# Up phase of a gated MLP: stored first products written back into the accumulating bank, first weights earlier, rows by halves

## The chip, the cores and the metric

One core of a Trainium2 chip. The metric is the device time of one execution in microseconds; the time before is the median of three runs, 2032.83 us (2030.95 to 2035.71).

## The reference

One layer of a decoder trunk over 1024 positions of 1024 channels in fp32: a token-mixing part (a conformer convolution branch and a Mamba-2 branch, gated and projected by `w_o`), a layer norm, a convolutional gated MLP, a layer norm. The change lies in the MLP and in the seams on both its sides:

```python
def conv_ffn(h, w_up, dw_w, dw_b, w_down):
    u = causal_dwconv(h @ w_up, dw_w, dw_b)      # 1024 -> 2 x 2816 columns, 3 taps
    gate, val = jnp.split(u, 2, axis=-1)
    return (jax.nn.silu(gate) * val) @ w_down    # 2816 -> 1024

h = layer_norm(DN_ALPHA * h + mix, ln1_g[l], ln1_b[l])
ffn = conv_ffn(h, w_ffn_up[l], ffn_dw_w[l], ffn_dw_b[l], w_ffn_down[l])
h = layer_norm(DN_ALPHA * h + ffn, ln2_g[l], ln2_b[l])
```

## The kernel before

Every fp32 product is made of three matmuls (`mm3`, lines 166 to 168): each operand is split into a rounded part (a ScalarE cast) and the rest (a VectorE subtraction), and three of the four cross products are added in one bank of PSUM. There are eight banks, four of tag "acc" (`bank(1)`) and four of tag "sm" (`bank(0)`).

The mixing part takes the positions in two halves, up to about 1350 us. Then come the stages of the change.

- `ffn_blocks` (to about 1391 us) opens the pool "trans" on the left side of the core's memory. Its first tiles are `ln1_g`, `ln1_b` and three buffers "row" of 4,096 bytes per partition each, then `h1raw` and the small `ts` tiles. `out_proj_pairs` projects the last four row blocks in two pairs and norms them (L717, L207, L227, L230); `block_sums` transposes each block (L758) and forms the sums and differences of blocks that a seven-product (Strassen-like) scheme needs, written into `h1b1`, `h1b2` and `h1s1` to `h1s3` (L763, L764; POOL does some of the sums, L788, L794).
- `up_first`: for the first eight pairs of columns (`LEAD = 8`) the two products that need only the early positions are made ahead, since they don't depend on the last rows: product with `b11`, copied out of the bank (L823) into a tile of the pool "firsts" (right side) and stored to `first_scr` in HBM, then the product with `b21` added onto the same bank, copied and stored again. Their weights pass through `weights()` (L152 to L155): a load into `wst` (three buffers, tag "st"), a cast and a split into `wsp` (three buffers).
- `up_rest` (about 1406 to 1794 us), 22 pairs. `up_weights` loads two weight tiles (`ra` L831 into "st", `rb` L836 into "raw", three buffers), forms four sums (L840 to L843) and splits (`split_pair`, L740, L741) into `wsp` (`w24`, `w10`) and the pool "up" (`w3`). Each pair then has five products of 12 matmuls (t2, t3, t1, t4, b22), and pairs from the ninth on the two first ones as well. In the first eight pairs the stored sums are loaded again (L867, L868), and three VectorE additions (L871, L877, L885) join them to what is in the banks; in the later ones everything accumulates in the bank and ScalarE copies it out (L860, L865, L875, L883). L878 and L880 form `uv` on VectorE in all pairs. Then a 3-tap convolution: a first tap on ScalarE into a tile "o" (L891, three buffers), two on VectorE (L895), SiLU (L905), the gating (L906), and for every second pair four sums (L920 to L923). The results go to HBM by POOL's queue (L916, L918, L924, L925).
- `down` (about 1794 to the end): seven products over eleven blocks each, weights through `load` (L979 and after) into `w_dn` tiles. `c3` and the 1024 rows of the residual (`rows`) take over the two big tiles. `load_rows` brings the rows by POOL's queue (L946); the first five `c3` blocks come by POOL's queue a second time (L982). `ln2`'s two rows are loaded by SP ahead of it all (L203).

The order on each engine is made by a planner from estimated times: among what is ready it takes what stands first in program order, where `high_priority(offset=n)` counts as n instructions earlier. A tile that lies where tiles of a closed pool lay waits for those tiles (`reuse_waits="tile"`). The pools stack up from the left and from the right side; "up" opens after "trans" has closed and so begins at the same address.

Of the kernel before, what the change touches and what calls it, by code (L numbers as in the profile page):

```python
# [8 lines left out]
F32 = mybir.dt.float32  # L9
F32R = mybir.dt.float32r  # L10
AF = mybir.ActivationFunctionType
ALU = mybir.AluOpType
# [4 lines left out]
P = 128  # L17
D = 1024
T = 1024
# [37 lines left out]
def kernel(  # L57
# [756 lines left out]

    def up_first(fp, bl, j):


        w = weights(wup[2 * j], f"ue{j}")
        ps = bank(1)
        for q, block in enumerate(("b11", "b21")):  # L820
            product(ps, lambda i: w[:, i, q * HALF : (q + 1) * HALF], bl[block], q == 0)
            f = fp.tile([P, HALF], F32, tag="first", bufs=4, name=f"first{q}_{j}")
            A.copy(f, ps)  # L823
            A.dma_start(first_scr[j][q], f)
# [23 lines left out]

    def up_rest(upp, us, bl, j, before):

        ue, w24, w10, w3 = up_weights(upp, j)
        ug, uv = us[2 * j % 3], us[(2 * j + 1) % 3]
        s = upp.tile([P, HALF], F32, tag="s", bufs=2, name=f"s{j}")
        early, late = slice(2, 2 + HALF), slice(2 + HALF, 2 + T)
        ps, pz = bank(1 if ue else 0), bank(0)
        if ue:
            product(ps, lambda i: ue[:, i, :HALF], bl["b11"], True)
            A.copy(s, ps)  # L860
            py = bank(1)
            product(py, lambda i: ue[:, i, HALF:], bl["b21"], True)
            V.tensor_tensor(out=ug[:, early], in0=s, in1=py, op=ALU.add)
            product(ps, lambda i: w24[:, i, :HALF], bl["t2"], False)
            A.copy(s, ps)  # L865
        else:
            SY.dma_start(s, first_scr[j][0])  # L867
            SY.dma_start(ug[:, early], first_scr[j][1])  # L868
            pu = bank(0)
            product(pu, lambda i: w24[:, i, :HALF], bl["t2"], True)  # L870
            V.tensor_tensor(out=s, in0=s, in1=pu, op=ALU.add)  # L871
        product(pz, lambda i: w3[:, i], bl["t3"], True)
        product(ps, lambda i: w10[:, i, :HALF], bl["t1"], not ue)
        if ue:
            A.copy(uv[:, late], ps)  # L875
        else:
            V.tensor_tensor(out=uv[:, late], in0=s, in1=ps, op=ALU.add)  # L877
        V.tensor_tensor(out=uv[:, late], in0=pz, in1=uv[:, late], op=ALU.subtract)  # L878
        product(pz, lambda i: w10[:, i, HALF:], bl["t4"], False)
        V.tensor_tensor(out=uv[:, early], in0=pz, in1=s, op=ALU.subtract)  # L880
        product(ps, lambda i: w24[:, i, HALF:], bl["b22"], False)
        if ue:
            A.copy(ug[:, late], ps)  # L883
        else:
            V.tensor_tensor(out=ug[:, late], in0=s, in1=ps, op=ALU.add)  # L885
        os = []
        j = j // 2 + j % 2 * NK
        for jj, u in ((j, ug), (NF + j, uv)):
            o = upp.tile([P, T], F32, tag="o", bufs=3, name=f"fo{jj}")
            wc = PC_FW + 3 * jj  # L890
            A.activation(  # L891
                out=o, in_=u[:, 2 : 2 + T], func=AF.Identity, scale=pc[:, wc + 2 : wc + 3]
            )
            for k in range(2):
                V.scalar_tensor_tensor(  # L895
                    out=o,
                    in0=u[:, k : k + T],
                    scalar=pc[:, wc + k : wc + k + 1],
                    in1=o,
                    op0=ALU.mult,  # L900
                    op1=ALU.add,
                )
            os.append(o)
# [22 lines left out]

    def down(upp, dp, g, b):

# [14 lines left out]

        def load_rows(ts):
            for t in ts:
                G.dma_start(rs[t], h1_scr[t * P : (t + 1) * P, :])  # L946

        E, L = slice(0, HALF), slice(HALF, D)

# [13 lines left out]
        def load(p, k):  # L963
# [12 lines left out]
            with tc.high_priority(offset=4000):  # L976
# [3 lines left out]
                if p == 0 and k < EARLY:  # L980
                    SY.dma_start(w_st, a11)
                    G.dma_start(c3[k], a11)  # L982
                elif p == 0:
# [77 lines left out]
        def four(t):  # L1061
            more(Y[t], rs[t], L, ALU.add)
            ln_part(dp, rs[t], sts[t], 1)
            ln_out(upp, t, rs[t], g, b, sts[t])

        def three(t):
            own(X[t], rs[4 + t], E, ALU.add)
            ln_part(dp, rs[4 + t], sts[4 + t], 0)
            ln_out(upp, 4 + t, rs[4 + t], g, b, sts[4 + t])

# [46 lines left out]
    with pool("trans") as tp:  # L1117
        bl = ffn_blocks(tp, qp, mixT)
    with pool("firsts", side="right") as fp:
        for j in range(LEAD):  # L1120
            up_first(fp, bl, j)
    upp = ctx.enter_context(pool("up"))
    us = [upp.tile([P, T + 32], F32, name=f"u{i}") for i in range(3)]
    for u in us:
        G.memset(u[:, :2], 0.0)
# [106 lines left out]
```

## Time and profile before

| | |
|---|---|
| runs | 2035.71, 2032.83, 2030.95 us; median 2032.83 |
| profiled execution | 2035.35 us, span 2033.6 us |
| TensorE busy | 1978.0 us (97%), mean granted clock 0.99 |
| VectorE, ScalarE, GpSimd busy | 1710.7 (84%), 1001.8 (49%), 171.9 us (8%) |
| HBM | 222.36 MB read, 49.55 MB written, 134 GB/s over the span |
| TensorE idle, 1400.5 to 1405.8 us | 5.3 us |
| TensorE waits on VectorE's L877 in the first eight pairs | 7.0 us in 3 |
| TensorE waits on ScalarE's L875 at 1804 us | 5.39 us in 1 |

PE is TensorE, PEld its weight loads, DVE VectorE, ACT ScalarE, POOL GpSimd, SP the queue that issues most loads. Times are microseconds from the start of the span. A row of the timeline gives start, duration, engine, line, operation, output and inputs, and in brackets the idle time before it and what ended it. A row of the groups gives count, busy time and mean nanoseconds, then the idle time ahead of them by releaser. A row of the waits gives engine, line, what it waited for, and total, number and longest.

### The profile page before, as it was taken

What the parts mean: (1) busy time and instruction counts of PE and PEld (TensorE: products, weight loads), DVE (VectorE), ACT (ScalarE), POOL (GpSimd) and SP (SyncE); (2) the same over time, 40 slices, a digit from 0 to 9 for tenths busy, and PEclk for the clock granted to TensorE, in tenths of its full rate; (3) what the DMA queues carried; (4) which work ended last, traced back from release to release, by engine and by line L of the source; (5) the groups of instructions that cost most, each with busy time, mean ns of one, the idle gap of its engine ahead of it and who ended that gap; (6) DMA issues with size and microseconds to landing.
All of it is one profiled execution on the core that took longest, in us unless ns stands there. A gap on an engine that the chain in (4) does not pass through costs nothing.

```text
span 2033.6 us, 24571 instructions
## 1 busy us (share of the span) xinstructions
PE 1978.0 (97%) x9164; PEld 1628.0 (80%) x9164; DVE 1710.7 (84%) x2285; ACT 1001.8 (49%) x1448; POOL 171.9 (8%) x141
## 2 busy tenths in 40 slices
PE   6999999999999999999999999998899999989998
PEld 6888887888788888888888888887778888777886
DVE  7599999989766869999998976596998788777868
ACT  4465654556453356665454645364334445443432
POOL 2010101001400000100100130010000000010000
PEclk9999999999999999999999999999999999999999
DMA  6212233332546522222423354565342232377563
GB/s 219 93 63 94 79 102 106 99 104 101 174 133 216 195 88 77 88 85 75 127 86 107 109 166 138 188 234 202 130 153 106 99 109 99 109 258 264 175 224 109
DMA packets 97303, 273.51 MB, mean 134 GB/s; under 512 B 11168, under 2 KB 11168, under 8 KB 97184
## 3 DMA queue, kind: packets, MB, share of 16 engines
q1 hardware_dynamic: 87696, 242.06, 35.9%
q0 software_dynamic: 7184, 25.69, 3.3%
q10 hardware_dynamic: 2304, 4.20, 0.6%
q8 instruction: 72, 1.18, 0.2%
q14 instruction: 47, 0.39, 0.1%
HBM read 222.36 MB, written 49.55 MB: 134 GB/s over the span
## 4 chain that ended last, share of the span: by engine, by line
PE 66%; DVE 24%; DMA 4%; issue 4%; ACT 1%; SPq 0%; DVEq 0%; ACTq 0%
PE acc L166 17%; PE acc L168 17%; PE acc L167 17%; DVE c L420 8%; PE sm L166 3%; PE sm L167 3%; PE sm L168 3%; DVE xbc L375 2%; DMA dr<-b_scr 1%; PE acc L357 1%; PE sm L534 1%; DVE fo L895 1%; DMA st_wo<-wo 1%; PE sm L515 1%; DVE w_so L155 1%
## 5 line engine op out<-in xcount | busy, mean ns | idle before, releaser
L420 DVE SCALAR_TENSOR_TENSOR c<-v,pc,c 128x512 f32<-128x512 f32 x480 | 375.3, 805 | 7.6 <-ACT c L409 6.1
L478 POOL TENSOR_TENSOR au<-seg_mv,head_of 128x1024 fp32r<-128x1024 f32 x32 | 76.3, 2383 | 962.2 <-PE sm L487 730.4
L166 PE MATMUL acc<-hT,w_c 128*128 128x512 f32 x352 | 141.1, 401 | 0.0
L167 PE MATMUL acc<-hT,w_c 128*128 128x512 f32 x352 | 140.7, 400 | 0.0
L168 PE MATMUL acc<-hT,w_c 128*128 128x512 f32 x352 | 138.5, 393 | 0.0
L895 DVE SCALAR_TENSOR_TENSOR fo<-u,pc,fo 128x1024 f32<-128x1024 f32 x88 | 111.5, 1279 | 8.5 <-ACT fo L891 7.8
L375 DVE SCALAR_TENSOR_TENSOR xbc<-u,pc,xbc 128x512 f32<-128x512 f32 x144 | 109.7, 774 | 0.7 <-ACT xbc L373 0.5
L167 PE MATMUL acc<-w_z,hT 128*128 128x512 f32 x256 | 100.9, 394 | 0.0
L166 PE MATMUL acc<-w_z,hT 128*128 128x512 f32 x256 | 100.9, 401 | 0.0
L168 PE MATMUL acc<-w_z,hT 128*128 128x512 f32 x256 | 100.7, 396 | 0.0
L1021 ACT CAST w_dn<-dr 128x1024 fp32r<-128x1024 f32 (+1 forms) x73 | 60.8, 842 | 77.7 <-DVE dr L951 31.5
L154 ACT CAST w_c<-st_c 128x1024 fp32r<-128x1024 f32 x50 | 52.5, 1051 | 86.8 <-PE acc L168 66.1
L1022 DVE TENSOR_TENSOR w_dn<-dr,w_dn 128x1024 fp32r<-128x1024 f32 (+1 forms) x73 | 69.6, 963 | 17.6 <-ACT w_dn L1021 17.5
L167 PEld LDWEIGHTS acc<-hT,w_c 128*128 128x128 f32 x352 | 66.2, 188 | 16.8 <-issue 3.8
L168 PEld LDWEIGHTS acc<-hT,w_c 128*128 128x128 f32 x352 | 66.1, 188 | 16.0 <-issue 2.6
L166 PEld LDWEIGHTS acc<-hT,w_c 128*128 128x128 f32 x352 | 66.1, 188 | 15.9 <-issue 2.6
L155 DVE TENSOR_TENSOR w_c<-st_c,w_c 128x1024 fp32r<-128x1024 f32 x47 | 60.6, 1289 | 20.2 <-ACT w_c L154 20.2
L166 PE MATMUL acc<-h1s,w_s 128*128 128x512 f32 x168 | 66.6, 397 | 5.7 <-ACT u L875 5.7
L166 PE MATMUL acc<-h1b,w_ue 128*128 128x512 f32 x176 | 68.9, 392 | 2.6 <-ACT w_ue L740 1.4
L166 PE MATMUL sm<-h1b,w_s 128*128 128x512 f32 x176 | 70.3, 400 | 0.0
L167 PE MATMUL sm<-h1b,w_s 128*128 128x512 f32 x176 | 70.3, 399 | 0.0
L168 PE MATMUL sm<-h1b,w_s 128*128 128x512 f32 x176 | 69.9, 397 | 0.0
(352 smaller groups left out, 5811.1 us busy)
## 6 DMA issues: line engine op xcount, KB each, us to landing
st_c<-wcol SPq DMA_DIRECT2D x50, 512.0 KB, 3.5
st_z<-wz SPq DMA_DIRECT2D x32, 512.0 KB, 3.4
st_wo<-wo SPq DMA_DIRECT2D x24, 512.0 KB, 3.8
ra<-wup SPq DMA_DIRECT2D x22, 512.0 KB, 3.6
rb<-wup SPq DMA_DIRECT2D x22, 512.0 KB, 3.4
t_scr<-fo POOLq DMA_DIRECT2D x22, 512.0 KB, 4.2
dr<-t_scr SPq DMA_DIRECT2D x44, 256.0 KB, 3.4
dr<-wdown SPq DMA_DIRECT2D x38, 256.0 KB, 3.8
```

Source lines behind the costliest of these rows:

```text
L154: A.copy(w[:, 0, :], st)
L155: (eng or V).tensor_tensor(out=w[:, 1, :], in0=st, in1=w[:, 0, :].bitcast(F32), op=ALU.subtract)
L166: TE.matmul(ps, wa(0), xa(0), start=start, stop=False, skip_group_check=more)
L167: TE.matmul(ps, wa(0), xa(1), start=False, stop=False, skip_group_check=more)
L168: TE.matmul(ps, wa(1), xa(0), start=False, stop=stop, skip_group_check=more)
L357: TE.matmul(ps[:, ts], w[:, i, k * P : (k + 1) * P], hT[:, j, k, ts], start=n == 0 and k == 0, stop=n == 2 and k == KD - 1,)
L375: V.scalar_tensor_tensor(out=o, in0=u[:, k : k + HALF], scalar=pc[:, wc + k : wc + k + 1], in1=o, op0=ALU.mult, op1=ALU.add,)
L420: V.scalar_tensor_tensor(out=accs[i], in0=v[:, k : k + HALF], scalar=pc[:, wc + k : wc + k + 1], in1=accs[i], op0=ALU.mult, op1=ALU.add,)
L478: G.tensor_tensor(out=au, in0=seg_mv[:, c, :].unsqueeze(1).to_broadcast([P, 8, P]), in1=head_of[:, g, :].unsqueeze(2).to_broadcast([P, 8, P]),
L895: V.scalar_tensor_tensor(out=o, in0=u[:, k : k + T], scalar=pc[:, wc + k : wc + k + 1], in1=o, op0=ALU.mult, op1=ALU.add,)
L1021: A.copy(w[:, 0, cs], src)
L1022: V.tensor_tensor(out=w[:, 1, cs], in0=src, in1=w[:, 0, cs].bitcast(F32), op=ALU.subtract)
```

## The change

- `up_first` copies its sums into the halves of the three `u` tiles of the pool "up" (`us[j % 3]`) instead of into "firsts", which is gone. "up" and the clearing of the `u` tiles move ahead of it.
- For j = 6 and 7 the weights are loaded and split by hand into two "o" tiles of "up" each, not into `wsp`. `up_weights(upp, 0)` is called ahead of them and its result handed to the first `up_rest`.
- In the first eight pairs ScalarE copies the stored first sum into the accumulating bank (`A.copy(ps, s)`), t2 is added onto it, and the rest goes as in the later pairs: L871, L877 and L885 become ScalarE copies. The loads of the stored sums get a priority of 2,500. `ps` is always an "acc" bank, and the bank `pu` is gone.
- "o" has four buffers instead of three.
- In `down` the rows are loaded by halves of columns, in four groups at k = 4 of products 0, 1, 2 and 4 (before: whole rows, two groups at k = 2 of 0 and 2). `ln2`'s rows come by POOL's queue with the third group, into "o" tiles. The first five `c3` blocks are copied on POOL from the tile just loaded, not loaded again.

```diff
-    def up_first(fp, bl, j):
-        w = weights(wup[2 * j], f"ue{j}")
+    def up_first(upp, us, bl, j):
+        if j < LEAD - 2:
+            t = weights(wup[2 * j], f"ue{j}")
+            w = [t[:, i, :] for i in range(2)]
+        else:
+            with tc.high_priority(offset=4000):
+                st = wst.tile([P, D], F32, tag="st", name=f"st_ue{j}")
+                SY.dma_start(st, wup[2 * j])
+                w = [upp.tile([P, D], F32R, tag="o", bufs=4, name=f"ue{i}_{j}") for i in range(2)]
+                A.copy(w[0], st)
+                V.tensor_tensor(out=w[1], in0=st, in1=w[0].bitcast(F32), op=ALU.subtract)
...
-            f = fp.tile([P, HALF], F32, tag="first", bufs=4, name=f"first{q}_{j}")
+            f = us[j % 3][:, 2 + q * HALF : 2 + (q + 1) * HALF]
             A.copy(f, ps)
             A.dma_start(first_scr[j][q], f)
...
-        ue, w24, w10, w3 = up_weights(upp, j)
+        ue, w24, w10, w3 = ws or up_weights(upp, j)
...
-        ps, pz = bank(1 if ue else 0), bank(0)
+        ps, pz = bank(1), bank(0)
...
-            product(ps, lambda i: w24[:, i, :HALF], bl["t2"], False)
-            A.copy(s, ps)
         else:
-            SY.dma_start(s, first_scr[j][0])
-            SY.dma_start(ug[:, early], first_scr[j][1])
-            pu = bank(0)
-            product(pu, lambda i: w24[:, i, :HALF], bl["t2"], True)
-            V.tensor_tensor(out=s, in0=s, in1=pu, op=ALU.add)
+            with tc.high_priority(offset=2500):
+                SY.dma_start(s, first_scr[j][0])
+                SY.dma_start(ug[:, early], first_scr[j][1])
+            A.copy(ps, s)
+        product(ps, lambda i: w24[:, i, :HALF], bl["t2"], False)
+        A.copy(s, ps)
         product(pz, lambda i: w3[:, i], bl["t3"], True)
-        product(ps, lambda i: w10[:, i, :HALF], bl["t1"], not ue)
-        if ue:
-            A.copy(uv[:, late], ps)
-        else:
-            V.tensor_tensor(out=uv[:, late], in0=s, in1=ps, op=ALU.add)
+        product(ps, lambda i: w10[:, i, :HALF], bl["t1"], False)
+        A.copy(uv[:, late], ps)
...
-        if ue:
-            A.copy(ug[:, late], ps)
-        else:
-            V.tensor_tensor(out=ug[:, late], in0=s, in1=ps, op=ALU.add)
+        A.copy(ug[:, late], ps)
...
-            o = upp.tile([P, T], F32, tag="o", bufs=3, name=f"fo{jj}")
+            o = upp.tile([P, T], F32, tag="o", bufs=4, name=f"fo{jj}")
...
-        def load_rows(ts):
-            for t in ts:
-                G.dma_start(rs[t], h1_scr[t * P : (t + 1) * P, :])
+        def load_rows(p):
+            t0, cs = {0: (0, E), 1: (0, L), 2: (4, L), 4: (4, E)}[p]
+            for t in range(t0, t0 + 4):
+                G.dma_start(rs[t][:, cs], h1_scr[t * P : (t + 1) * P, cs])
+            if p == 2:
+                for n, start in (("g", RW_2G), ("b", RW_2B)):
+                    r = upp.tile([P, D], F32, tag="o", bufs=4, name=f"ln2_{n}")
+                    G.dma_start(r, prow[start : start + D].partition_broadcast(P))
+                    gb.append(r)
...
-                    G.dma_start(c3[k], a11)
+                    G.tensor_copy(c3[k], w_st)
...
-                if k == 2 and p in (0, 2):
-                    load_rows(range(2 * p, 2 * p + 4))
+                if k == 4 and p in (0, 1, 2, 4):
+                    load_rows(p)
...
-    with pool("firsts", side="right") as fp:
-        for j in range(LEAD):
-            up_first(fp, bl, j)
     upp = ctx.enter_context(pool("up"))
     us = [upp.tile([P, T + 32], F32, name=f"u{i}") for i in range(3)]
     for u in us:
         G.memset(u[:, :2], 0.0)
+    for j in range(LEAD):
+        if j == LEAD - 2:
+            ws = up_weights(upp, 0)
+        up_first(upp, us, bl, j)
     before = None
     for j in range(NF):
-        before = up_rest(upp, us, bl, j, before)
+        before, ws = up_rest(upp, us, bl, j, before, ws), None
     ffn_stack.close()
     dp = ctx.enter_context(pool("down", side="right"))
-    g, b = row(dp, RW_2G, D, "ln2_g"), row(dp, RW_2B, D, "ln2_b")
-    down(upp, dp, g, b)
+    down(upp, dp)
```

More of the change, by code (lines that the diff above doesn't have):

```diff
@@ L813, in ffn_blocks @@
         }
-    def up_first(fp, bl, j):
-        w = weights(wup[2 * j], f"ue{j}")
+    def up_first(upp, us, bl, j):
[9 more added lines that the diff above has]
+                V.tensor_tensor(out=w[1], in0=st, in1=w[0].bitcast(F32), op=ALU.subtract)
         ps = bank(1)
         for q, block in enumerate(("b11", "b21")):
-            product(ps, lambda i: w[:, i, q * HALF : (q + 1) * HALF], bl[block], q == 0)
-            f = fp.tile([P, HALF], F32, tag="first", bufs=4, name=f"first{q}_{j}")
+            product(ps, lambda i: w[i][:, q * HALF : (q + 1) * HALF], bl[block], q == 0)
+            f = us[j % 3][:, 2 + q * HALF : 2 + (q + 1) * HALF]
             A.copy(f, ps)
@@ L847, in up_weights, with up_rest @@
         return ue, w24, w10, w3
-    def up_rest(upp, us, bl, j, before):
-        ue, w24, w10, w3 = up_weights(upp, j)
+    def up_rest(upp, us, bl, j, before, ws):
+        ue, w24, w10, w3 = ws or up_weights(upp, j)
         ug, uv = us[2 * j % 3], us[(2 * j + 1) % 3]
@@ L925, in up_rest, with down @@
         G.dma_start(t41_scr[j - NK], a)
-    def down(upp, dp, g, b):
+    def down(upp, dp):
         LAST, EARLY = 8, 5
@@ L1063, in four @@
             ln_part(dp, rs[t], sts[t], 1)
-            ln_out(upp, t, rs[t], g, b, sts[t])
+            ln_out(upp, t, rs[t], *gb, sts[t])
         def three(t):
@@ L1068, in three @@
             ln_part(dp, rs[4 + t], sts[4 + t], 0)
-            ln_out(upp, 4 + t, rs[4 + t], g, b, sts[4 + t])
+            ln_out(upp, 4 + t, rs[4 + t], *gb, sts[4 + t])
         products = (
```

1 line of the change is left out of this document (added).

## The prediction

> **What bounds the kernel now.** I read the page's busy shares first, then the busy time of each engine by stretches, then TensorE's waits in the stretches where it was idle.
>
> ```profile
> span 2033.6 us, 24571 instructions
> PE 1978.0 (97%) x9164; PEld 1628.0 (80%) x9164; DVE 1710.7 (84%) x2285; ACT 1001.8 (49%) x1448; POOL 171.9 (8%) x141
> ```
>
> TensorE is the bound over the whole span, so only its idle or slow stretches can be won. The change touches three places; these are their stretches (columns: window, then busy us of PE, PEld, DVE, ACT, POOL, granted clock, DMA share, GB/s):
>
> ```profile
> 1350.00:1400.50 50.50, 49.34 (x224) 40.13 (x222) 39.21 (x55) 27.58 (x46) 9.14 (x9) 1.00 0.61 218
> 1400.50:1405.80 5.30, 0.04 (x1) 0.00 (x0) 3.59 (x6) 2.86 (x5) 0.00 (x0) 0.92 0.89 307
> 1405.80:1411.50 5.70, 5.66 (x13) 4.46 (x14) 5.03 (x7) 1.99 (x2) 0.00 (x0) 0.50 0.74 231
> 1405.80:1531.00 125.20, 117.07 (x479) 93.77 (x480) 113.62 (x141) 45.69 (x46) 6.61 (x12) 0.95 0.41 143
> 1430.00:1531.00 101.00, 93.31 (x390) 74.79 (x389) 96.66 (x118) 39.88 (x40) 6.61 (x12) 0.97 0.44 154
> 1600.00:1700.00 100.00, 100.00 (x439) 81.99 (x438) 83.36 (x94) 50.22 (x60) 5.87 (x11) 1.00 0.31 108
> 1800.00:1810.00 10.00, 5.73 (x18) 4.64 (x19) 6.89 (x6) 3.79 (x5) 0.54 (x1) 0.66 0.34 134
> 1830.00:1840.00 10.00, 7.50 (x29) 5.48 (x28) 5.29 (x9) 3.32 (x6) 1.07 (x2) 0.92 1.03 403
> ```
>
> In 1600 to 1700 a 512-column matmul takes 100/439 = 0.228 us. By that measure the eight first pairs (8 x 60 = 480 matmuls in 1405.8 to 1531) need 109.3 us and take 125.2: 15.9 too many. VectorE is busy 96.66 of 101 us there, against 83 of 100 later. Before them lie 5.3 idle us, and the 5.7 us after these run at half clock (13 matmuls, 2.9 us lost). In the down phase 1800 to 1810 has 18 matmuls and 1830 to 1840 has 29, for 44 each: 5.9 and 3.4 us lost.
>
> **a. First columns: the new staging place.** Before, `up_first` copied its sums into the pool "firsts" on the right side, which nothing else held. Now it copies into `us`, the first 3 x 4,224 bytes per partition of the pool "up". That pool opens where "trans" has just closed, and trans begins with `ln1_g`, `ln1_b` (4,096 bytes each) and three `row` buffers. So `us[0]` lies on `ln1_g` and the start of `ln1_b`, `us[1]` on `ln1_b` and the head of a row buffer, `us[2]` on row buffers. These are read until the last layer norm of `out_proj_pairs`:
>
> ```profile
> 1353.34 0.39 PE L166 MATMUL acc<-h1b,w_ue 128*128 128x512 f32 x1
> 1356.81 0.58 ACT L823 COPY first<-acc 128x512 f32<-128x512 f32 x1
> 1360.06 1.21 DVE L155 TENSOR_TENSOR w_ue<-st_ue,w_ue 128x1024 fp32r<-128x1024 f32 x1
> 1365.49 1.18 DVE L155 TENSOR_TENSOR w_ue<-st_ue,w_ue 128x1024 fp32r<-128x1024 f32 x1
> 1371.95 1.22 DVE L155 TENSOR_TENSOR w_ue<-st_ue,w_ue 128x1024 fp32r<-128x1024 f32 x1
> 1373.07 1.03 PE L758 MATMUL sm<-ident,r 128*128 128x128 f32 x8
> 1373.08 1.27 DVE L230 SCALAR_TENSOR_TENSOR r<-r,rs_o,ln_b 128x1024 f32<-128x1024 f32 x1
> 1383.08 0.17 POOL L1125 MEMSET u<- 128x2 f32 x3
> 1390.26 0.69 DVE L764 TENSOR_TENSOR h1b<-ts,h1b 128x512 fp32r<-128x512 f32 x1 [0.69 <-ACT h1b L763]
> ```
>
> The first sum was copied out at 1356.81; its new place is free at 1373.08 + 1.27 = 1374.4. The two weight splits at 1365.49 and 1371.95 belong to columns 3 and 4, whose buffer (three in `wsp`) is not free until column 0 is done, so they fall behind and the norm ends 2.3 us sooner, at 1372.1; with the copy (0.58) TensorE can go on at about 1372.8. Until then it can do the first product of columns 0, 1 and 2 (three weight buffers; the third split ends at 1361.3). Before, (1372.8 - 1353.34) / (12 x 0.228 = 2.73) = 7.1 products were done by then, so 4.1 are late: 11.3 us. One of two groups of eight row transposes (1.03 us) moves into the gap: +10.3. The gap is over 5 us, so by the 1405.8 row half clock follows: +2.9. Sum of a: **+13.2**.
>
> **b. From first columns to pairs.** The gap comes from the weights of pair 0, which could take a `wsp` buffer only when the last columns gave theirs back:
>
> ```profile
> 1397.48 0.50 PE L166 MATMUL acc<-h1b,w_ue 128*128 128x512 f32 x1 [1.17 <-ACT first L823]
> 1405.84 0.79 PE L166 MATMUL sm<-h1s,w_s 128*128 128x512 f32 x1 [5.30 <-ACT w_s L740]
> ```
>
> Columns 6 and 7 now use two "o" tiles each, pair 0's weights take `wsp` buffers after columns 3 to 5, some 8 us ahead of need (`wup` loads for it move ahead of two others on SP; at a DMA share of 0.61 that costs nothing). Columns 6, 7 make the same casts and splits; their "o" tiles lie on `h1raw`, free before 1391, and are due after 1400. So the 5.3, the half clock (2.9) and the wait of 1.17, which pair 0's products can fill, go: **-9.4**.
>
> **c. The first eight pairs.** Removed from VectorE are the three additions of each pair, added to ScalarE are four copies of 512 columns:
>
> ```profile
> L871 DVE TENSOR_TENSOR s<-s,sm 128x512 f32<-128x512 f32 x8 | 5.5, 683 | 0.1
> L877 DVE TENSOR_TENSOR u<-s,sm 128x512 f32<-128x512 f32 x7 | 4.8, 684 | 0.6 <-PE sm L168 0.6
> L885 DVE TENSOR_TENSOR u<-s,sm 128x512 f32<-128x512 f32 x7 | 4.8, 684 | 2.8 <-PE sm L168 2.6
> L860 ACT COPY s<-acc 128x512 f32<-128x512 f32 x9 | 5.3, 589 | 12.6 <-PE acc L168 12.6
> L891 ACT ACTIVATE fo<-u,pc 128x1024 f32<-128x1024 f32 x14 | 16.0, 1151 | 13.4 <-DVE fo L923 8.7 <-DMA t_scr<-fo 3.6 <-DVE u L880 0.6
> PE sm L166 <- DVE u L877: 7.0, 3, 3.9
> SPq L868 <- DVE fo L895: 38.7, 6, 10.6
> ```
>
> VectorE loses 24 x 0.684 = 16.4 us: 113.6 becomes 97.2, or 89% of 109. ScalarE gains 32 x 0.59 = 18.9 (the copy into PSUM has no row; 0.58 to 0.62 are the nearest): 45.7 becomes 64.6, 59%. TensorE's order in a pair is now that of pairs 8 to 21, which run with no idle at VectorE 83%. Of the 15.9 us too many, 2.9 are b's half clock; of the other 13.0 I let 3.5 stay, since VectorE remains fuller than later: **-9.5** (ends: -13, and +2 in the rival below). The copy into the bank waits for the load of `s` alone, which SP issues earlier (up to 2,500 instructions); on SP the loads of `ra`, `rb` stand behind it and behind `u`'s, which waited 38.7 us in six times already without TensorE waiting for a load. I cost that at nothing: weights come a pair ahead; without this cover a late load is some 3 us each.
>
> **d. Start of the down phase.**
>
> ```profile
> 1786.23 2.71 POOL L982 DMA_DIRECT2D c<-wdown  x5 [17.06 <-PE acc L168]
> 1788.93 0.54 POOL L918 DMA_DIRECT2D b_scr<-fo  x1
> 1798.77 1.15 ACT L891 ACTIVATE fo<-u,pc 128x1024 f32<-128x1024 f32 x1 [4.06 <-DMA b_scr<-fo]
> 1801.51 1.15 ACT L891 ACTIVATE fo<-u,pc 128x1024 f32<-128x1024 f32 x1 [1.59 <-DMA t_scr<-fo]
> 1799.96 5.34 DVE L895 SCALAR_TENSOR_TENSOR fo<-u,pc,fo 128x1024 f32<-128x1024 f32 x4 [5.56 <-ACT fo L891]
> 1803.65 0.57 ACT L875 COPY u<-acc 128x512 f32<-128x512 f32 x1
> 1804.27 0.79 PE L166 MATMUL acc<-h1s,w_s 128*128 128x512 f32 x1 [5.39 <-ACT u L875]
> 1811.90 4.25 POOL L946 DMA_DIRECT2D rows<-h_scr  x8 [3.97 <-PE sm L168]
> ```
>
> ScalarE stood for an "o" buffer until a store landed, and TensorE for the copy L875 behind it. A fourth buffer lets the first L891 go at once; the second still waits for a store, so L875 comes about 2 us earlier, and less half clock follows. Five loads of 256 KB are gone (1.3 MB, 3.3 us at 403 GB/s) and the two `ln2` rows (1 MB) come later, which shortens the crowd that delays 1830 to 1840. The eight row loads become sixteen halves, 8.6 us of POOL's issue for 4.25, the same 4 MB: POOL issued all eight at once, for p=2 too, so I don't count on the new spacing. I take **-4** of the 9.3 lost; ends: -9 and +5.
> The five POOL copies of 512 columns that replace the loads have no row; this pair shows the nearest thing, an addition of that size beside VectorE:
>
> ```profile
> 1367.30 1.24 DVE L227 SCALAR_TENSOR_TENSOR r<-r,mv_o,ln_g 128x1024 f32<-128x1024 f32 x1
> 1367.35 2.34 POOL L794 TENSOR_TENSOR ts<-h1raw,ts 128x512 f32<-128x512 f32 x1 [8.83 <-DVE h1s L764]
> 1368.52 2.25 DVE L227 SCALAR_TENSOR_TENSOR r<-r,mv_o,ln_g 128x1024 f32<-128x1024 f32 x1
> 1381.84 1.30 POOL L794 TENSOR_TENSOR ts<-h1raw,ts 128x512 f32<-128x512 f32 x1 [4.61 <-DVE h1s L764]
> ```
>
> The same work took 1.0 longer on both when they met. A copy is between the 0.55 of the issue that it replaces and 1.3; for the sum I take them as hidden, since VectorE idles 5.56 us ahead of 1799.96.
>
> **The sum.** +13.2 - 9.4 - 9.5 - 4 = -9.7, or 2025.7 against the profiled execution's 2035.35, which is 2.5 above the median. From the median of 2032.83: **2023**.
>
> **Rivals.**
> - The staging place doesn't bind (TensorE finds other products, or the norm is done sooner): a is nothing, -22.9, 2010. For: the third split is at 1360, near the norm. Against: 1356.81 and 1374.4 are 17 us apart.
> - ScalarE takes VectorE's place in the pairs: the copies that free the banks stand behind L891, which waited 8.7 + 3.6 = 12.3 us for "o" buffers there. If TensorE waits all of it and one half clock (2.9), c is -13 + 15 = +2 and the total +1.8: 2035. Against: the fourth buffer, and pairs 8 to 21, which have those copies already.
> - POOL's copies meet VectorE's two-input work at 1786 to 1794 and put L918 behind them: 5 x 1.0 on VectorE, and up to 5 x 1.3 - 2.7 = 4 us on the store that ScalarE waits for. With both on the path d is +5, the total -0.7: 2032. The Trainium skill, "SBUF — State Buffer", section "Who interferes with whom", says that a VectorE instruction with two SBUF inputs contends with a GpSimd instruction that reads SBUF, and that whoever is first blocks the other. The row at 1368.52 agrees with it (2.25 for 1.24).
> - Slower: `us` comes free only when all of trans is done, at 1390.26 + 0.69 = 1391.0. TensorE then resumes 18.8 us later than I have it: total +9.1, 2042. It decides from the point where the first copy starts 9.7 us later than 1372.2, slower by more than 0.2% from 13.8 later (1386). Against: `us` was cleared at 1383.08, before trans' last read, so the waits are by tile; for: `us[1]` and `us[2]` also wait for the store and transposes of a row.
>
> **How the numbers follow.** Chances: the forecast 0.48, staging free 0.15, ScalarE 0.16, POOL 0.08, slower 0.13. 0.2% is 4.1 us, about what this measurement can tell from nothing. Faster: 0.48 + 0.15 = 0.63; same: 0.16 + 0.08 = 0.24; slower 0.13. The likeliest alone spans 2016 (c -12, d -9) to 2029 (c -6, d -2). The range takes in the ScalarE and POOL cases and the better half of the free case: 2011 to 2036.
>
> **What would show it.** For a: a TensorE gap of 6 to 10 us between 1361 and 1373, released by ScalarE's copy of first sums, half clock after it. For b: no gap and clock 1.00 where the pairs start, near 1410. For c: ScalarE copies in place of L871, L877, L885, VectorE under 92%, the ninth pair within 114 us of the first. For d: no wait of over 4 us behind L891. I am wrong if the gap in a is missing or over 15 us, or if waits on ScalarE take the place of those on VectorE in c.

## The result, and the profile after

The changed kernel takes **2043.47 us** (median of five runs, 2042.5 to 2050.02) against 2035.1 for the kernel before beside it (2030.95 to 2037.42): a ratio of 1.005 [1.003, 1.007], slower by 8.4 us where I forecast 9.7 less. The profiled execution took 2043.57 us, 8.2 more than the one of before.

The page, its first lines:

```profile
span 2041.9 us, 24575 instructions
PE 1976.6 (97%) x9164; PEld 1625.8 (80%) x9164; DVE 1696.7 (83%) x2261; ACT 1018.5 (50%) x1480; POOL 179.4 (9%) x151
```

VectorE has 14 us less work and ScalarE 17 more, as meant; TensorE works as long as before and stands longer. The stretches of the change; the last two lie where the same work stands that the kernel before does at 1800 to 1810 and 1830 to 1840, some 10 us later here (window, then busy us of PE, PEld, DVE, ACT, POOL, granted clock, DMA share, GB/s):

```profile
1363.00:1385.00 22.00, 3.98 (x18) 3.13 (x16) 19.69 (x30) 8.40 (x17) 4.95 (x6) 0.67 0.15 59
1385.00:1391.00 6.00, 5.96 (x14) 4.71 (x15) 0.23 (x1) 1.39 (x3) 0.00 (x0) 0.51 0.85 279
1423.60:1541.30 117.70, 111.87 (x481) 89.59 (x480) 90.82 (x104) 57.84 (x72) 6.59 (x12) 1.00 0.42 142
1600.00:1700.00 100.00, 95.79 (x417) 77.55 (x416) 76.82 (x90) 43.06 (x54) 5.84 (x11) 1.00 0.28 100
1811.00:1821.00 10.00, 10.00 (x46) 8.29 (x45) 8.29 (x8) 4.37 (x5) 0.98 (x2) 1.00 0.40 133
1840.00:1850.00 10.00, 8.57 (x38) 6.78 (x37) 5.58 (x10) 5.04 (x9) 0.68 (x2) 1.00 1.04 395
```

Two stretches are worse than before: 22 us at the first columns with 18 matmuls, 16 of them small row transposes, with half clock behind them, and the later pairs, where 1600 to 1700 had 439 matmuls and now has 417. The seam to the down phase has 46 matmuls for 18 and runs full; a little behind it there are 38 for 29, still short of 44. What TensorE waited for from 1350 to 1860:

```profile
PE acc L166 <- ACT u L831: 11.0, 1, 11.0
PE acc L166 <- ACT w_ue L740: 9.1, 7, 1.4
PE sm L758 <- DVE r L230: 7.1, 1, 7.1
PE acc L166 <- ACT acc L876: 3.8, 2, 2.2
```

The 11.0 and the 7.1 are one gap, cut in two by the row transposes (rows from the timeline of after; here and below rows between them are left out):

```profile
1370.54 3.54 PE L758 MATMUL sm<-ident,r 128*128 128x128 f32 x16 [7.10 <-DVE r L230]
1370.92 1.27 DVE L230 SCALAR_TENSOR_TENSOR r<-r,rs_o,ln_b 128x1024 f32<-128x1024 f32 x1
1383.88 0.62 ACT L763 CAST h1b<-ts 128x512 fp32r<-128x512 f32 x1 [2.51 <-DVE ts L794]
1384.41 1.07 ACT L831 COPY u<-acc 128x512 f32<-128x512 f32 x2
1385.04 0.80 PE L166 MATMUL acc<-h1b,w_ue 128*128 128x512 f32 x1 [10.96 <-ACT u L831]
```

The first copy of a first sum (L831) follows directly on the last cast of trans (L763), 12 us after the norm's last read (L230, done at 1372.2).

To see where each kernel spends its time I count the MLP's matmuls (lines 166 to 168) from 0 in the order in which TensorE runs them, and take the time from the start of one to the start of another: up-phase matmuls 0, 84, 192 (the first pair begins), 252, 672 (past the first eight pairs), 1764, 1847 (the last), then number 132 of the down phase. From there on all kernels take the same 149.6 us for the next 660. The runs named are those of the experiments below, each by one profiled execution.

| us between matmuls | 0-84 | 84-192 | 192-252 | 252-672 | 672-1764 | 1764-1847 | to down 132 |
|---|---|---|---|---|---|---|---|
| before | 19.3 | 33.2 | 16.6 | 108.9 | 251.7 | 28.2 | 33.2 |
| after | 45.8 | 24.8 | 13.8 | 103.9 | 259.8 | 21.4 | 30.3 |
| e1 own pool, some overlap | 45.6 | 25.3 | 13.6 | 104.2 | 258.4 | 21.5 | 32.7 |
| e2 before + staging | 45.5 | 24.5 | 13.8 | 108.4 | 251.7 | 29.1 | 31.8 |
| e3 before + ScalarE | 19.1 | 29.6 | 15.3 | 108.9 | 258.1 | 26.9 | 33.2 |
| e4 before + down | 19.0 | 33.2 | 15.3 | 108.0 | 251.6 | 24.1 | 33.2 |
| e8 the same, four "o" | 19.1 | 33.2 | 15.3 | 104.1 | 258.1 | 21.4 | 34.2 |
| e5 after, free place | 19.0 | 33.7 | 13.8 | 104.7 | 259.9 | 21.4 | 33.2 |
| e7 e5 with VectorE | 19.0 | 33.6 | 13.9 | 101.8 | 258.0 | 21.4 | 32.5 |
| e6 e5 + halves | 19.1 | 33.1 | 13.8 | 102.7 | 249.3 | 22.3 | 32.6 |
| e9 e6 with VectorE | 19.1 | 35.1 | 13.9 | 102.1 | 251.3 | 22.4 | 32.5 |
| e11 e6, s on ScalarE | 19.4 | 33.3 | 13.9 | 101.9 | 252.6 | 22.3 | 34.0 |
| e12 e6, s on GpSimd | 19.1 | 33.7 | 13.8 | 102.6 | 249.6 | 22.5 | 30.1 |
| e10 e9 without b | 19.2 | 26.2 | 13.8 | 103.1 | 251.3 | 22.4 | 30.9 |
| e15 e6 without b | 19.1 | 26.3 | 13.9 | 105.6 | 248.8 | 22.4 | 31.0 |
| e16 e15, s on GpSimd | 19.1 | 26.2 | 13.9 | 102.8 | 248.8 | 22.4 | 32.9 |
| e13 before, two first buffers | 19.2 | 26.3 | 13.8 | 108.3 | 251.7 | 28.0 | 33.7 |
| e14 after + halves | 45.8 | 24.8 | 13.8 | 102.7 | 249.3 | 22.3 | 34.5 |

From before to after: +26.5, -8.4, -2.8, -5.0, +8.1, -6.8, -2.9, in all +8.7, against 8.2 between the two profiled executions. Two things go with the table. The sixteen row transposes take some 1.6 us between matmuls; they lie in 0-84 in after, e1, e2 and e14, and in 84-192 everywhere else, so like for like the first two differences are +24.9 and -6.8. And e4 runs the instructions of before in the same order on every engine up to the down phase, yet differs by 1.3 us in 192-252 and by 0.9 in 252-672 (and reaches matmul 0 3.4 us sooner): a difference of a microsecond in one stretch tells nothing by itself.

### The profile page after: what moved, and what is told of

It is laid out like the page before. It is cut to its first block, busy times and chain, and to the rows that moved or that the text cites. A ratio compares the mean times of both kernels' runs of the same rounds, so it can differ in the third digit from the quotient of the medians.

```text
span 2041.9 us, 24575 instructions
## 1 busy us (share of the span) xinstructions
PE 1976.6 (97%) x9164; PEld 1625.8 (80%) x9164; DVE 1696.7 (83%) x2261; ACT 1018.5 (50%) x1480; POOL 179.4 (9%) x151
## 4 chain that ended last, share of the span: by engine, by line
PE 73%; DVE 19%; DMA 4%; issue 3%; ACT 1%; SPq 0%; POOL 0%; DVEq 0%; ACTq 0%; POOLq 0%
PE acc L166 19%; PE acc L167 19%; PE acc L168 19%; DVE c L420 6%; PE sm L166 3%; PE sm L167 3%; PE sm L168 3%; PE sm L534 2%; PE acc L357 1%; DVE xbc L375 1%; DMA dr<-b_scr 1%; PE sm L515 1%; PE sm L192 1%; PE sm L523 1%; DVE w_c L155 1%
## 5 line engine op out<-in xcount | busy, mean ns | idle before, releaser
L166 PE MATMUL acc<-h1s,w_s 128*128 128x512 f32 x264 | 102.9, 394 | 5.1 <-ACT acc L876 3.8
L168 PE MATMUL acc<-h1s,w_s 128*128 128x512 f32 x264 | 103.0, 391 | 0.0
L167 PE MATMUL acc<-h1s,w_s 128*128 128x512 f32 x264 | 102.9, 390 | 0.0
L1030 ACT CAST w_dn<-dr 128x1024 fp32r<-128x1024 f32 (+1 forms) x73 | 61.1, 843 | 77.2 <-DVE dr L960 35.1
L166 PE MATMUL acc<-h1b,w_ue 128*128 128x512 f32 x160 | 64.3, 403 | 20.1 <-ACT u L831 11.0
L740 ACT CAST w_s<-rb 128x1024 fp32r<-128x1024 f32 x22 | 23.1, 1049 | 113.4 <-PE sm L168 68.8
```

What stands on the lines that cost most here:

```text
L166: TE.matmul(ps, wa(0), xa(0), start=start, stop=False, skip_group_check=more)
L167: TE.matmul(ps, wa(0), xa(1), start=False, stop=False, skip_group_check=more)
L168: TE.matmul(ps, wa(1), xa(0), start=False, stop=stop, skip_group_check=more)
L1030: A.copy(w[:, 0, cs], src)
```

## The experiments

My theories after the result: the gap comes from where the staging tile lies (rival: from ScalarE's and VectorE's work); the loss in the later pairs comes from the cast of `ue`; part c is smaller than I took it.

**e1, the u tiles in a pool of their own on the right side, staging through the second and third.**

```diff
-    us = [upp.tile([P, T + 32], F32, name=f"u{i}") for i in range(3)]
+    up_u = ffn_stack.enter_context(pool("upu", side="right"))
+    us = [up_u.tile([P, T + 32], F32, name=f"u{i}") for i in range(3)]
-            f = us[j % 3][:, 2 + q * HALF : 2 + (q + 1) * HALF]
+            f = us[1 + j % 2][:, 2 + q * HALF : 2 + (q + 1) * HALF]
```

> The changed kernel, but the three u tiles lie in a pool of their own on the right side, where trans reaches only the first of them, and the first sums are staged in the other two. Theory (the staging place makes the 22 us gap before the second product of column 0): no TensorE wait on L831 there, the first column's copy near 1356, kernel 20 to 26 us shorter than the changed one, 2018 to 2024. Rival (the gap comes from pair 0's weights and the hand-made splits standing in ScalarE's and SP's queues): the gap stays, 2040 to 2044.

2040.65 us, ratio 1.0029 [1.0019, 1.004]. The gap stayed, 10.8 us behind L831. The pool's first tile still overlaps 2.7 KB of two `ts` buffers of trans; the two tiles used overlap nothing. Yet (timeline of e1):

```profile
1382.11 0.62 ACT L763 CAST h1b<-ts 128x512 fp32r<-128x512 f32 x1 [2.51 <-DVE ts L794]
1382.63 1.07 ACT L831 COPY u<-acc 128x512 f32<-128x512 f32 x2
1383.57 0.17 POOL L1132 MEMSET u<- 128x2 f32 x3 [5.78 <-DVE h1b L764]
```

So it isn't the tile's own address, nor the clearing of the `u` tiles, which came behind the copy here. The copy is late by its place in ScalarE's queue.

**e2, e3, e4: one part each on the kernel before.** e2 takes the staging in `us`, with "up" opened ahead of the columns, and nothing else; e3 the first eight pairs' ScalarE copies and the loads' priority; e4 the down phase's edits with three "o" buffers.

> The kernel before with one part alone: the first sums staged in the u tiles, which open on the place of trans; nothing else moved. Theory (staging place): TensorE stands still from about 1363 to 1385, and the gap of 5.3 us at the start of the pairs stays: 18 to 28 us slower than before, 2053 to 2063. Rival (moved weights): no difference, 2031 to 2039.

> The kernel before with one part alone: in the first eight pairs ScalarE writes the stored sum into the bank and copies the results out. Theory (VectorE bounds these pairs): pairs 1 to 8 are 8 to 13 us shorter, and from pair 12 TensorE waits some 1.5 us on the w_ue cast in every second pair as in the changed kernel (5 times, +7): total -1 to -6, 2029 to 2034. Rival (the late waits come from the fourth o buffer, not from these copies): no such waits, 2022 to 2027. Rival (ScalarE in VectorE's place gains nothing): 2035 or more.

> The kernel before with one part alone: rows by halves, ln2 rows by POOL's queue, the first five c3 blocks copied on POOL; o keeps three buffers, and the up phase is as before. Theory (the seam at 1800 gained 10 us by the fourth o buffer): 5.4 us wait on L875 stays, gain under 3 us, 2032 to 2036. Rival (1.3 MB fewer loads at 1786 free the store that ScalarE waits for): wait gone, 2025 to 2030.

e2: 2047.06 us, 1.0057 [1.0041, 1.0073]; the staging alone makes the gap, and it has the short stretches 84-192 and 192-252 of after without part b. The 5.3 us before pair 0, which I had expected to stay, are gone with it, and so it is 13 us slower than before and not 18 or more. e3: 2033.54, 0.9996 [0.9984, 1.0007]; the first pairs gain nothing (108.9 for 108.9), and the later ones lose 6.4 us with five waits for `w_ue`; what makes up for it is a shorter gap ahead of pair 0 (84-252: 44.9 for 49.8), whose t3 now goes first. So the total falls into my range for another reason than mine. In the first pairs no wait for VectorE's additions is left, but others have come. TensorE's waits for the copy into the bank, and what ended ScalarE's idle time ahead of that copy (L868 in e3):

```profile
PE acc L166 <- ACT acc L868: 9.2, 5, 2.8
  DMA s<-first_scr: 9.4, 6
```

The load of `s` came late there. e4: 2026.14, 0.9951 [0.9936, 0.9966]; the down phase's edits alone beat both kernels. TensorE's wait for L875 fell from 5.7 us to 3.1. The table finds 4.1 us from matmul 1764 on; for the rest of the 8 I have no cause, since ahead of the down phase both kernels run the same instructions in the same order.

**e5, the free place.** As e1, but the first u tile stays in "up", so that the right-side pool (8,448 bytes) overlaps no tile of trans:

```diff
-    us = [up_u.tile([P, T + 32], F32, name=f"u{i}") for i in range(3)]
+    us = [(up_u if i else upp).tile([P, T + 32], F32, name=f"u{i}") for i in range(3)]
```

> The changed kernel, but the second and third u tile lie in a pool of their own on the right side, at an address that no tile of trans uses, and the first columns' sums go through these two by turns. Theory: the gap of the first columns comes from the address. As long as the pool of the staging tile overlaps any tile of trans, the copy of the first sum is put behind all of trans' copies on ScalarE (it then started at 1384.4); with a place that is free from the start it stands ahead of them, as in the kernel before. Then the stretch from the first matmul of the first columns to the 84th takes about 20 us as before, not 45; of the changed kernel's other parts the transition (-9.7), the first pairs (-5), the late pairs (+8) and the start of the down phase (-10) stay, and the time is 2018 (2014 to 2022). Rival: the copy is late because ScalarE and VectorE are busy with the norm and the transposes, wherever it goes; then TensorE again stands until about 1385, and the time stays at 2036 or above.

2025.66 us, 0.9959 [0.9944, 0.9973]. The gap is gone (19.0 us for 0-84). ScalarE's timeline:

```profile
1352.32 0.61 ACT L763 CAST h1b<-ts 128x512 fp32r<-128x512 f32 x1
1352.84 0.58 ACT L831 COPY u<-acc 128x512 f32<-128x512 f32 x1
1353.81 0.59 ACT L763 CAST h1s<-sm 128x512 fp32r<-128x512 f32 x1 [0.39 <-DVE ts L789]
```

Now the copy stands between casts of trans. The stretch 84-192 is at 33.7, though, and not at the 24.8 of after, with 1.6 us of the difference for the transposes; that explains the 8 us above what I expected.

**e6, the casts of `ue` in halves, on e5.**

```diff
-            ue = None if j < LEAD else split_pair(wsp, r1, f"ue{j}")
+            ue = None
+            if j >= LEAD:
+                ue = wsp.tile([P, 2, D], F32R, tag="w", name=f"w_ue{j}")
+                for h in (slice(0, HALF), slice(HALF, D)):
+                    A.copy(ue[:, 0, h], r1[:, h])
+                    V.tensor_tensor(out=ue[:, 1, h], in0=r1[:, h], in1=ue[:, 0, h].bitcast(F32), op=ALU.subtract)
```

> As the run with the free staging place, and the cast and the remainder of the full weights (ue) of pairs 8 to 21 are made in two halves of 512 columns each, so that the first product of the pair needs only the first half of the cast. Theory: the loss of about 8 us in the late pairs is the wait of TensorE for this cast (8.4 us in six of seven pairs, 1.4 to 1.6 each), because the buffer comes free only four matmuls before the product. With halves the instruction order also comes out with only one such pair; the waits for w_ue fall under 2 us and the time is 8 us under that of the run with the free place: about 2010. Rival: the late loss is VectorE and ScalarE being full, and the wait only shows where it surfaces; then other waits take its place and the gain is under 3 us.

2014.97 us, 0.9911 [0.9893, 0.9929]: 10.7 less than e5, nearly all of it in 672-1764 (259.9 to 249.3). One of the waits it removes, in the timeline of the changed kernel:

```profile
1576.00 0.39 PE L168 MATMUL sm<-h1b,w_s 128*128 128x512 f32 x1
...
1576.42 1.05 ACT L740 CAST w_s<-rb 128x1024 fp32r<-128x1024 f32 x1 [9.72 <-PE sm L168]
1576.68 0.39 PE L168 MATMUL acc<-h1s,w_s 128*128 128x512 f32 x1
1577.37 1.04 ACT L740 CAST w_ue<-ra 128x1024 fp32r<-128x1024 f32 x1
1578.47 0.50 PE L166 MATMUL acc<-h1b,w_ue 128*128 128x512 f32 x1 [1.40 <-ACT w_ue L740]
```

ScalarE waits 9.72 us for TensorE to finish with a buffer, then makes two casts of 1.05 us in a row, and TensorE has some three matmuls (0.7 us) left to do until the second is ready. Seven of the fourteen later pairs have this wait. The order too comes out different with halves, so the shorter cast and the new order aren't told apart.

**e7, e5 with VectorE's additions as before; e8, e4 with four "o" buffers.**

> As the run with the free staging place, but the stored first products are added by VectorE in the first eight pairs as before the change, instead of being written into the accumulating bank by ScalarE. It measures part c by itself, without the staging gap. Theory: part c gains 5 to 8 us in the first eight pairs and costs 3 to 4 us in the late ones, where its tight order leaves six late pairs waiting for w_ue and this kernel four; so this kernel is 1 to 5 us slower than the run with the free place. Rival 1: my first estimate of part c (-9.5) holds, and this kernel is 8 us or more slower. Rival 2: part c is worth nothing, the difference is under 1 us or has the other sign.

> The kernel before with the down phase of the changed one and four o buffers in place of three; up phase otherwise as before. The same with three buffers gave 2026.1. Theory: the fourth buffer gives the start of the down phase another 5.7 us (from the 1764th matmul of the up phase to the end 231 us instead of 236.6), and it also lets the pairs run in the tight order in which every second late pair waits for w_ue: four waits of 1.5 us, +6. Together the time is 2026 (2023 to 2029), with waits for w_ue of 5 to 6 us. Rival: the late waits come from ScalarE's accumulation alone; then they are under 2 us here, and the time is 2020.

e7: 2020.09 us, 0.9936 [0.9919, 0.9953], 5.6 *faster* than e5: ScalarE's way is a loss there, 2.9 us in 252-672 and 1.9 in 672-1764. That is rival 2. The first eight pairs of e7, and below them of e5:

```profile
1402.80:1518.50 115.70, 113.64 (x482) 89.27 (x481) 110.48 (x140) 46.71 (x49) 6.62 (x12) 1.00 0.43 148
```

```profile
1402.30:1520.80 118.50, 113.20 (x481) 90.79 (x480) 95.31 (x112) 59.12 (x74) 6.62 (x12) 0.99 0.44 148
```

VectorE is busy 95% in the faster one, 80% in the slower. e8: 2027.06, 0.9971 [0.9959, 0.9983], as expected: the fourth buffer gains 3.9 us in 252-672 and 1.7 from 1764 on, and loses 6.5 in the later pairs, where five waits for `w_ue` sum to 6.5 us. So that order comes with the buffer alone and with ScalarE's copies alone (e3). L891's idle time in 1400 to 1530 of e8:

```profile
L891 ACT ACTIVATE fo<-u,pc 128x1024 f32<-128x1024 f32 x14 | 16.0, 1152 | 8.9 <-DVE u L885 4.0 <-DMA t_scr<-fo 1.8 <-DVE u L880 1.5
```

Before, 12.3 of its 13.4 us were for "o" buffers (L923 and the store); here the store's 1.8 is what is left of them.

**e9 to e12, on e6.** e9 uses VectorE's additions; e10 is e9 without part b (columns 6 and 7 through `weights()`, pair 0's weights after them); e11 and e12 issue the load of `s` on ScalarE's and on GpSimd's queue.

> The free staging place and the ue casts by halves (2015.0 with ScalarE's accumulation), with the stored first products added by VectorE as before the change. Theory: with the late waits gone, part c is left with its price in the first eight pairs alone, where ScalarE's copy into the bank waits for the load of s (3.2 us); VectorE's way took 115.7 us for them against 116.5 to 118.5. So this kernel is 1 to 3 us faster, 2012 to 2014. Rival: part c gains once the late waits are gone, and this kernel is 3 us or more slower.

> As the run with the free place, the halves and VectorE's additions, but without part b: the weights of columns 6 and 7 again take the common buffers, and pair 0's weights come after the last column. Theory: the gap of 5.3 us before pair 0 and the half clock behind it (2.9) come back, and the wait of 2.7 us for column 6's cast in the first columns (and its half clock) goes, so part b is worth 2 to 4 us and this kernel is that much slower. Rival: part b is worth the 9.4 us that I predicted, and this kernel is 8 us or more slower.

> The free staging place and the halves, with ScalarE's accumulation, and the load of s issued on ScalarE's queue instead of SP's, where it stands behind the load into u that waits for VectorE (28 to 30 us in six times). Theory: the waits of TensorE for the copy into the bank (3.2 us in two) come from the late load of s; they go, and the time is 2 to 3 us under 2015. Rival: on ScalarE's queue the load waits for VectorE to give back the s buffer and holds up the copies behind it; then TensorE waits for ScalarE by as much or more, and the time is 2015 or above.

> As the last one, but the load of s is issued on GpSimd's queue. Theory: the same, the waits for the copy into the bank go and the time is 2 to 3 us under 2015. Rival: on GpSimd the load stands behind the stores of finished pairs, which wait for VectorE (179 us in eleven times over the phase), and comes later than on SP: the wait for the copy grows over 3.2 us and the time is above 2015.

e9: 2016.17 us, 0.9909 [0.9894, 0.9924], no different from e6. e10: **2009.5**, 0.9878 [0.9865, 0.9892]. Undoing part b gained 6.7 us; both my theory and the rival had the sign wrong. It lies in 84-192: 35.1 with b, 26.2 without. ScalarE in e9:

```profile
1387.03 0.62 ACT L763 CAST h1b<-ts 128x512 fp32r<-128x512 f32 x1 [0.47 <-DVE ts L794]
...
1387.56 1.04 ACT L825 CAST ue<-st_ue 128x1024 fp32r<-128x1024 f32 x1
```

The cast of column 6's weights goes into an "o" tile of "up" and stands behind the last cast of trans, as the staging copies did. By the sizes of the tiles ahead of it this tile lies on two `row` buffers, whose last readers, the row transposes, were done 11 us sooner:

```profile
1373.95 1.91 PE L758 MATMUL sm<-ident,r 128*128 128x128 f32 x16
```

TensorE waits 2.7 for the cast and 1.5 for its remainder, and the clock granted in 1390 to 1397 is 0.52. e11: 2017.15, 0.9921 [0.9909, 0.9934], the rival: waits for the copy into the bank 4.1 us in place of 3.2. e12: 2012.35, 0.9896 [0.9882, 0.991]; that wait falls to 2.6, but most of the 2.6 us gained on e6 lies outside the first pairs (32.6 to 30.1 in the last stretch), so the theory isn't shown by it, though its time came true.

**e13, the kernel before with two first buffers.** This leaves the two pools "up" and "firsts" without their overlap of 2.4 KB.

```diff
-            f = fp.tile([P, HALF], F32, tag="first", bufs=4, name=f"first{q}_{j}")
+            f = fp.tile([P, HALF], F32, tag="first", bufs=2, name=f"first{q}_{j}")
```

> The kernel before with two buffers for the first sums in place of four; nothing else. The pool of the first sums then ends at the top of the right side and no longer overlaps the pool up by 2.4 KB. Theory: the 5.3 us before pair 0 came from that overlap, not from wsp buffers that are late: as long as the two pools overlap, the cast of pair 0's s3 (ready at 1391.6) stands behind the last copy of a first sum on ScalarE (1400.6). Without the overlap it stands ahead of it; the gap and the half clock go, 7 us, less up to 3 us for the fewer buffers: 2027 (2025 to 2030). Rival, as I predicted it: the weights of pair 0 wait for wsp buffers of the last columns; then the gap of 5.3 us stays and the time is 2034 or above.

2023.6 us, 0.9942 [0.9927, 0.9957], 1.4 us below my range. The gap before pair 0 is gone by one digit. ScalarE before, then with two buffers:

```profile
1400.58 0.58 ACT L823 COPY first<-acc 128x512 f32<-128x512 f32 x1 [3.15 <-PE acc L168]
...
1401.56 0.62 ACT L740 CAST w_s<-s 128x512 fp32r<-128x512 f32 x1 [0.40 <-ACT first L823]
```

```profile
1390.63 0.63 ACT L740 CAST w_s<-s 128x512 fp32r<-128x512 f32 x1
...
1396.79 0.59 ACT L823 COPY first<-acc 128x512 f32<-128x512 f32 x1 [0.87 <-DMA first_scr<-first]
...
1398.09 0.59 ACT L823 COPY first<-acc 128x512 f32<-128x512 f32 x1 [0.71 <-DMA first_scr<-first]
```

The cast of pair 0's `s3` stood behind the last copy out of "firsts" and now stands ahead of it; the `wsp` buffers are the same in both.

**e14, the changed kernel with halves; e15, e6 without part b; e16, e15 with the load of `s` on GpSimd's queue.**

> The changed kernel with one edit: the casts and remainders of ue in pairs 8 to 21 in halves. Theory: the waits of every second late pair for w_ue (9.1 us in seven) go, and the kernel is 8 to 10 us faster than the changed one: 2034 (2032 to 2036), about the time of the kernel before. Rival: the late loss has another cause, and the time stays above 2040.

> The free staging place, the halves, part b undone (2009.5 with VectorE's additions), with ScalarE's accumulation in the first eight pairs. It measures part c where neither the staging nor the late waits nor the casts of columns 6 and 7 disturb. Theory: part c is worth nothing there (2015.0 against 2016.2 with part b): 2008 to 2012, with 3 us of waits for the copy into the bank. Rival 1: it is worth a good part of the -9.5 I predicted: 2005 or less. Rival 2: the waits for the load of s make it a loss: 2013 or more.

> As the last one, with the load of s issued on GpSimd's queue (which gave 2012.35 for 2015.0 with part b). Theory: the wait for the copy into the bank falls or goes and the kernel is 2 to 3 us under the last one: about 2007, the fastest here. Rival: the load comes later on GpSimd without part b's earlier order; then the time is as in the last one or above.

e14: 2033.69 us, 0.9996 [0.9987, 1.0006]: 9.8 less than the changed kernel; the waits for `w_ue` fell from 9.1 us to 0.3 and 672-1764 by 10.5, so its late loss goes with these casts. e15: 2008.02, 0.9869 [0.9854, 0.9884]; e16: 2007.86, 0.9868 [0.9852, 0.9885], with e15 and e10 the fastest here; the intervals of the three overlap, and the 2 to 3 us that I expected of e16 didn't come. Part c has no worth in sum that these runs could tell (e15 against e10: +2.5 in 252-672, -2.5 in 672-1764).

## Why the prediction was wrong, point by point

**a, +13.2 predicted; +26.5 in 0-84, +24.9 without the transposes.** The step that failed is the place "free at 1373.08 + 1.27 = 1374.4", and from it "TensorE can go on at about 1372.8". TensorE went on at 1385.0. The gap's start, the weight splits that fall behind and the half clock after it (0.51 in 1385 to 1391) were as I had them; but I put the copy's start at the tile's last reader. What set it was the order that the planner had written for ScalarE: the copy stands behind the last cast of trans as long as some part of the pool of its tile overlaps trans (after, e1, e2) and ahead of it when none does (e5), though in e1 the tile itself was free; its row names no wait. That is the "slower" rival in effect. That its 2042 lies so near the 2043.5 measured is luck: it has the first copy at 1391.0 where 1384.4 was measured, and it lacks the loss in the later pairs. Against it I had set the clearing of `us` at 1383.08, ahead of trans' last read, as a sign that waits go by tile. That row told of GpSimd, which had finished with trans by then; it said nothing on ScalarE's order.

**b, -9.4 predicted; -6.8, the transposes left out, and -2.8 in the next two stretches.** The size was right, the cause wrong, so that was luck. "The weights of pair 0, which could take a `wsp` buffer only when the last columns gave theirs back": e13 loses the gap with the same buffers, and e2 without part b. The staging removes it as a side effect, since the pool "firsts", which overlapped "up", is gone. Part b itself is hidden by the gap of a in the changed kernel (24.8 against e2's 24.5), and with a free place it costs 7 us (e9 against e10).

**c, -9.5 predicted; -5.0 in 252-672, of which c has none.** The step that failed is "of the other 13.0 I let 3.5 stay, since VectorE remains fuller than later": I took a busy share of 96% for the limit. e7 runs faster at 95% than e5 at 80%. What TensorE waited for on VectorE (7.0 us at L877) came from something else in good part, for a fourth "o" buffer halves it with all additions left on VectorE (3.5 us in e8). The gain is that of the fourth "o" buffer (e8: 108.0 to 104.1), which I had booked under d alone, although the L891 row that I quoted shows 12.3 us of waiting for "o" in these very pairs. ScalarE's copies are worth 0.0 (e3) to a loss of 2.9 (e5 against e7). A second step failed with it, the load of `s`, "I cost that at nothing": TensorE waits for the copy behind it 3.8 us in the changed kernel (L876) and 9.2 in e3, where these waits take the place of those on VectorE.

**Not in the sum: +8.1 in 672-1764.** I argued that pairs 8 to 21 "run with no idle" and took them as fixed. An edit ahead of them can change their order: the staging (e2: 251.7) and two first buffers (e13: 251.7) leave it as it was, but two of this change's edits, ScalarE's copies (e3) and the fourth "o" buffer (e8), each bring the order that waits for `w_ue`.

**d, -4 predicted; -9.7 from 1764 on.** Without the fourth buffer it is -4.1 (e4), with it -5.8 (e8). The step was "the second still waits for a store": with four buffers no L892 in 1795 to 1812 waits for one. The other 3.9 us between e8 and after lie in the last stretch, which scatters from 30.1 to 34.5 between kernels that share their down phase. What goes with it in good part is one wait of TensorE for the cast of a weight block, which ScalarE starts when a load from `b_scr` lands: 1.0 us in e12, 1.4 in after, 4.0 in e8. Why the load is late by more in one kernel than in another is open. The POOL rival's contention shows, off the path, where the copies (L991) run beside VectorE (timeline of after):

```profile
1801.12 1.28 DVE L907 SCALAR_TENSOR_TENSOR fo<-fo,pc,fo 128x1024 f32<-128x1024 f32 x1
1801.36 1.52 POOL L991 COPY c<-dr 128x512 f32<-128x512 f32 x1 [12.35 <-PE acc L168]
1802.82 0.61 POOL L991 COPY c<-dr 128x512 f32<-128x512 f32 x1
1802.92 1.58 DVE L741 TENSOR_TENSOR w_s<-ra,w_s 128x1024 fp32r<-128x1024 f32 x1
1803.38 1.60 POOL L991 COPY c<-dr 128x512 f32<-128x512 f32 x1
1804.43 1.09 DVE L921 TENSOR_TENSOR fo<-fo,fo 128x512 f32<-128x512 f32 x1
1804.92 1.07 POOL L991 COPY c<-dr 128x512 f32<-128x512 f32 x1
1815.42 0.62 POOL L991 COPY c<-dr 128x512 f32<-128x512 f32 x1 [6.52 <-DMA dr<-wdown]
```

The last of these copies runs while VectorE idles and takes 0.62; L741 takes 1.21 elsewhere, L923, of the same shape as L921, 0.68. Whichever begins inside an instruction of the other engine takes longer, and each time by about what was left of that one: L741 by 0.37 with 0.51 of a copy left, the copy at 1803.38 by 1.0 with 1.1 of L741 left. The Trainium skill, "SBUF — State Buffer", section "Who interferes with whom", says that a VectorE instruction with two SBUF inputs contends with a GpSimd instruction that reads SBUF and that the order of issue decides who blocks; these rows agree. A copy thus cost a VectorE instruction 0.4 us and not the 1.0 of the rival, and TensorE has no wait there.

Open: by which of its rules the planner holds back a pool's tiles, and why it falls into the order that waits for `w_ue`; shown are only the orders and what changes them. Open too is what part c would be worth with the load of `s` in time.

## What to carry to other kernels

When an edit moves a tile into another pool, look at what that pool's area overlaps and where the instruction then stands in its engine's queue, not only at the last reader of the bytes: 2.4 KB of overlap cost 10 us, and no wait in the trace named them. A busy share near 100% on an engine (95% here) doesn't make it the limit; its rows of idle time, and who waits for it, do. Where one planner orders the whole phase, an edit in its first third can cost in the last, so the stretches that aren't edited belong in the sum with a price of their own.

## What was not expected of the hardware

The copy from SBUF into a bank (L876) took 0.587 us, as much as one out of a bank (medians of 0.574 to 0.589 for L868, L878, L881): a bound from the nearest rows was good. A GpSimd copy of 128x512 took 0.61 to 0.62 us where no VectorE instruction with two inputs in SBUF was running as it began, and 1.07 to 1.60 in the three cases where one was.
